# A 416-byte pad at the start of SBUF's left side in a one-core transformer layer

## Chip, core and metric

The kernel runs on one core of one Trainium2 chip. The metric is the device time of one execution in microseconds (us); a smaller number is better. The core's engines are TensorE (PE; its weight loads are shown apart as PEld), VectorE (DVE), ScalarE (ACT), GpSimd (POOL) and SyncE (SP, which issues most of the DMAs). SBUF, the on-chip memory, is addressed here by bytes within a partition; a tile takes the same bytes in all 128 partitions.

## The reference

One layer of a hybrid trunk, sequence 512, width 1024, all in float32:

```python
h = rms_norm(x, norm_mix)
proj = h @ w_in                       # 1024 x 8192: pool, lru, q, k, v, three gates
gates = sigmoid(g_logits + b_gate)
y_pool = pool_mixer(u_pool)           # causal means over 2/4/8/16, a map per group of 256
y_lru = rglru_mixer(u_lru)            # conv of width 4, two block-diagonal gates, a scan
y_sb = stick_breaking_attention(rms_norm(q), rms_norm(k), v)   # 8 heads of 128
merged = gates[0]*(y_pool @ w_branch[0]) + gates[1]*(y_lru @ w_branch[1]) \
       + gates[2]*(y_sb @ w_branch[2])
x = x + merged @ w_out
h2 = rms_norm(x, norm_ffn)
x = x + (silu(h2 @ w_ffn_gate) * (h2 @ w_ffn_up)) @ w_ffn_down   # d_ff 2816
```

## The kernel before

**Precision.** Every large product is done in split float32: each operand is the sum of a high part (rounded to the format float32r) and a low part (the rest), and TensorE does three matmuls, high by high, high by low and low by high, that add up in PSUM. A weight tile is loaded (`raw`, `qw` or `w`), ACT writes its high part (`whi` or `wh`, lines 92 and 1109), DVE subtracts and writes the low part (`wlo` or `wl`, lines 93 and 1110). The helper `mm3` (lines 215 to 218) issues the three matmuls; in the products of q, k, v line 654 does it, in the feed-forward part line 1119.

**A matmul's operands.** The first operand of `nc.tensor.matmul(ps, stationary, moving)` is loaded into the array beforehand; the second streams through it, 512 or 256 columns. In the profile an instruction reads `out<-moving,stationary`.

**Stages.** (1) Gates of branch 0 from the unnormalised input `hu`. (2) The normalised input is written as `HH` (high) and `HL` (low); gates of branch 1 and the lru projection, `HH`/`HL` moving. (3) q, k and v by a seven-product scheme (Strassen's kind), in which blocks of `HH`/`HL` (for three of the seven products) or of sums of them (`hT1` to `hT4`, for the other four) are stationary and the weights move; gates of branch 2 between. (4) The pool projection, with `HH`/`HL` moving, and the branch projections (`ps_br`), between which the attention of the eight heads is done in small tasks. (5) The last branch and the output projection (`ps_out`), whose moving operands are `mth` and `mtl`. (6) The feed-forward part: two chunks directly (`ps_fg`, `ps_fu`), seven more by seven 256-wide products each (`ps_y`, `ps_x`), then the down projection, partly direct (`ps_d`), partly by seven products (`ps_dy`, `ps_dx`).

**What sets the order.** The program is written out in order and each engine works its own queue. `weights()` makes the split weights ready three chunks ahead of their use; a list of small tasks (`bg`, `abg`) is worked off one or two at a time between half chunks. Semaphores keep data and buffers safe. No order depends on an address.

**Where buffers lie.** Tile pools are stacked. From the low end ("left") come the constants `cst`, then `mp`, `wp`, and above these `ap0` in stages 1 to 3, `sp` and `ap1` in stages 4 and 5, `gp` in stage 6. From the high end ("right") come `hp`, which holds `HH` and `HL`, and after it, in the same place, `cor`, which holds `mth` and `mtl` and later the raw weight tiles `w` and the normalised blocks `hn` of the feed-forward part. The places in the code, by line:

```python
# L67 to L72
    cst = ctx.enter_context(tc.tile_pool(name="cst", bufs=1))
    mp = ctx.enter_context(tc.tile_pool(name="mp", bufs=4))
    wp = ctx.enter_context(tc.tile_pool(name="wp", bufs=3))
    ...
    hp = hstack.enter_context(tc.tile_pool(name="hp", bufs=1, side="right"))
# L215 - L218
    def mm3(ps, lh, ll, rh, rl, start, stop, skip=False):
        nc.tensor.matmul(ps, lh, rh, start=start, stop=False, skip_group_check=skip)
        nc.tensor.matmul(ps, lh, rl, start=False, stop=False, skip_group_check=skip)
        nc.tensor.matmul(ps, ll, rh, start=False, stop=stop, skip_group_check=skip)
# L942
    cor = ctx.enter_context(tc.tile_pool(name="cor", bufs=8, side="right"))
```

The tiles of `mp`, `wp`, `ap0`, `sp`, `ap1`, `gp`, `hp` and `cor` are multiples of 512 bytes long, so all buffers of one side begin at the same residue modulo 512; in the built program this is 64 on the left and 480 on the right. The small tiles of `cst` (identity, ones, mask, scale columns) have residues of their own.

Of the kernel before, what the change touches and what calls it, by code (L numbers as in the profile page):

```python
# [8 lines left out]
F32 = mybir.dt.float32  # L9
# [7 lines left out]
P = 128  # L17
# [13 lines left out]
KD = 4  # L31
H = S // 2
AHEAD = 200
NAW, NAT, NAB = 8, 8, 13
NSP = 44
NLD = 12
# [24 lines left out]
def layer_kernel(ctx: ExitStack, tc: tile.TileContext, x, xt, vecs, w_in, w_pool, w_rg, w_ig,  # L61
# [5 lines left out]
    cst = ctx.enter_context(tc.tile_pool(name="cst", bufs=1))  # L67
# [131 lines left out]
    def emit_next():  # L199
# [4 lines left out]
        key, make = specs[i]  # L204
        with tc.high_priority(AHEAD if i > 3 else 0):
            ready[key] = make(str(i))
# [16 lines left out]
    def vcol(name, i=0):  # L223
        o = VOFF[name] + i
        return vt[:, o:o + 1]

    warm = cst.tile([P, S], BF16, tag="warm", name="warm")
    dve.memset(warm, 1.0)
    idn = cst.tile([P, P], F32, tag="idn", name="idn")
# [1077 lines left out]
```

## Time and profile before

| | us |
|---|---|
| median of 3 runs (lowest, highest) | 957.63 (956.97, 958.15) |
| the profiled execution's time | 956.69 |
| its span, first to last instruction | 954.9 |
| PE busy | 941.5 (99%) |
| PEld busy | 802.7 (84%) |
| DVE busy | 703.5 (74%) |
| ACT busy | 493.7 (52%) |
| POOL busy | 43.1 (5%) |

Busy times are shares of the span. PE's busy time is a union of modelled durations: a matmul is shown from its start to the end of its drain, and the next one starts before that, so the spacing of starts says more than the duration. In a row of instructions stand line, engine, operation, `out<-in`, shape and count, then the sum of busy time and the mean of one in ns, then idle time of the engine before them and what ended it. In a row of the timeline stand the start in us from the span's start, the duration in us, and the instruction. In the chain of work that ended last a piece has its start, its length, and the number of instructions merged in it. The granted TensorE clock was 0.999 of full speed over the span.

### The profile page before, as it was taken

How to read it: one execution, taken by the hardware profiler on the slowest of the kernel's cores; microseconds unless marked ns; L12 is line 12 of the kernel's file. 1: busy time of each engine (PE TensorE's matmuls, PEld its weight loads, DVE VectorE, ACT ScalarE, POOL GpSimd, SP SyncE). 2: the span in 40 equal slices, each digit the busy share in tenths (PEclk: the TensorE clock that was granted, in tenths of full speed). 3: DMA queues.
4: the chain of work that ended last, by engine and by line, in shares of the span. 5: the costliest groups of instructions: out<-in, count | busy, mean ns of one | idle time of the engine just before them, and what ended most of it. 6: DMA issues, size and time to landing. Idle time of an engine off the chain costs nothing.

```text
span 954.9 us, 13025 instructions
## 1 busy us (share of the span) xinstructions
PE 941.5 (99%) x5090; PEld 802.7 (84%) x5090; DVE 703.5 (74%) x876; ACT 493.7 (52%) x664; POOL 43.1 (5%) x71
## 2 busy tenths in 40 slices
PE   8899999999999999999999999999999999999998
PEld 5787778788888888788788878889999999988898
DVE  6597677978696599865865554699888887787464
ACT  5567779445755466654543223555555555652232
POOL 1100000131121000000000000000000000000000
PEclk9999999999999999999999999999999999999999
DMA  8474343661713933165432234345533334523001
GB/s 269 138 260 130 111 136 129 199 204 58 224 65 138 297 117 121 63 178 165 146 101 88 89 114 153 108 122 145 150 93 89 111 95 129 166 98 111 1 27 63
DMA packets 127790, 124.12 MB, mean 130 GB/s; under 512 B 7280, under 2 KB 107632, under 8 KB 127728
## 3 DMA queue, kind: packets, MB, share of 16 engines
q1 hardware_dynamic: 123840, 109.13, 36.9%
q0 software_dynamic: 3888, 14.16, 4.4%
q8 instruction: 40, 0.66, 0.3%
q14 instruction: 22, 0.18, 0.1%
HBM read 107.01 MB, written 16.25 MB: 129 GB/s over the span
## 4 chain that ended last, share of the span: by engine, by line
PE 91%; DVE 5%; ACT 2%; DMA 1%; issue 1%; SPq 0%; POOL 0%; DVEq 0%; ACTq 0%; POOLq 0%
PE ps_y L1119 11%; PE ps_q L654 9%; PE ps_x L1119 8%; PE ps_br L216 4%; PE ps_br L218 4%; PE ps_br L217 4%; PE ps_gate L217 4%; PE ps_gate L218 4%; PE ps_gate L216 4%; PE ps_d L216 3%; PE ps_d L218 3%; PE ps_d L217 3%; PE ps_dy L1119 2%; PE ps_dx L1119 2%; PE ps_out L216 2%; PE ps_lru L217 2%
## 5 line engine op out<-in xcount | busy, mean ns | idle before, releaser
L92 ACT ACTIVATE whi<-raw 128x1024 fp32r<-128x1024 f32 x93 | 98.3, 1058 | 159.0 <-PE ps_br L217 44.8
L93 DVE TENSOR_TENSOR wlo<-raw,whi 128x1024 fp32r<-128x1024 f32 x93 | 113.6, 1221 | 78.7 <-ACT whi L92 74.2
L1109 ACT ACTIVATE wh_S<-w_S 128x1024 fp32r<-128x1024 f32 x44 | 46.6, 1061 | 58.7 <-PE ps_y L1119 27.2
L1110 DVE TENSOR_TENSOR wl_S<-w_S,wh_S 128x1024 fp32r<-128x1024 f32 x44 | 53.6, 1221 | 13.7 <-ACT wh_S L1109 13.6
L1109 ACT ACTIVATE wh<-w 128x1024 fp32r<-128x1024 f32 x33 | 35.0, 1060 | 50.8 <-issue 13.4
L93 DVE TENSOR_TENSOR wlo<-qw,whi 128x1024 fp32r<-128x1024 f32 x36 | 43.9, 1221 | 20.5 <-ACT whi L92 20.2
L1110 DVE TENSOR_TENSOR wl<-w,wh 128x1024 fp32r<-128x1024 f32 x33 | 40.3, 1222 | 18.9 <-ACT wh L1109 18.9
L92 ACT ACTIVATE whi<-qw 128x1024 fp32r<-128x1024 f32 x36 | 38.0, 1056 | 30.4 <-PE ps_q L654 17.1
L216 PE MATMUL ps_gate<-HH,whi 128*128 128x512 f32 x128 | 50.9, 397 | 0.0
L218 PE MATMUL ps_gate<-HH,wlo 128*128 128x512 f32 x128 | 50.8, 397 | 0.0
L217 PE MATMUL ps_gate<-HL,whi 128*128 128x512 f32 x128 | 50.7, 396 | 0.0
L216 PE MATMUL ps_d<-ah,whi 128*128 128x512 f32 x112 | 43.6, 391 | 0.0
L217 PE MATMUL ps_d<-al,whi 128*128 128x512 f32 x112 | 43.6, 389 | 0.0
L218 PE MATMUL ps_d<-ah,wlo 128*128 128x512 f32 x112 | 43.6, 389 | 0.0
L1097 DVE TENSOR_TENSOR w_S<-w,w 128x1024 f32<-128x1024 f32 x22 | 26.9, 1222 | 3.4 <-PE ps_d L217 2.9
L218 PEld LDWEIGHTS ps_gate<-HH,wlo 128*128 128x128 f32 x128 | 24.1, 188 | 5.8
L217 PEld LDWEIGHTS ps_gate<-HL,whi 128*128 128x128 f32 x128 | 24.1, 188 | 5.7
L216 PEld LDWEIGHTS ps_gate<-HH,whi 128*128 128x128 f32 x128 | 24.1, 188 | 5.6
L1097 DVE TENSOR_TENSOR w_S<-w,w_S 128x1024 f32<-128x1024 f32 x22 | 26.9, 1223 | 0.6
L872 DVE TENSOR_TENSOR_SCAN E<-K,zero 128x511 f32<-128x511 f32 (+3 forms) x32 | 25.5, 813 | 1.5 <-ACT K L867 1.3
L216 PE MATMUL ps_out<-mth,whi 128*128 128x512 f32 x64 | 25.4, 398 | 0.9 <-DVE g L299 0.9
L216 PE MATMUL ps_gate<-hu,whi 128*128 128x512 f32 x64 | 25.2, 394 | 1.0 <-ACT whi L366 0.7
(638 smaller groups left out, 3047.8 us busy)
## 6 DMA issues: line engine op xcount, KB each, us to landing
raw<-in_w_in_dram SPq DMA_DIRECT2D x39, 512.0 KB, 4.1
qw<-in_w_in_dram SPq DMA_DIRECT2D x24, 512.0 KB, 4.6
raw<-in_w_branch_dram SPq DMA_DIRECT2D x24, 512.0 KB, 3.4
w<-in_w_ffn_gate_dram SPq DMA_DIRECT2D x36, 256.0 KB, 3.5
w<-in_w_ffn_up_dram SPq DMA_DIRECT2D x36, 256.0 KB, 4.2
raw<-in_w_ffn_down_dram SPq DMA_DIRECT2D x14, 512.0 KB, 3.5
qd<-r POOLq DMA_DIRECT2D x12, 512.0 KB, 3.4
at<-qd SPq DMA_DIRECT2D x24, 256.0 KB, 5.2
```

The costliest lines, as they stand in the source:

```text
L92: act(hi, raw, AF.Copy)
L93: dve.tensor_tensor(lo, raw, hi.bitcast(F32), ALU.subtract)
L216: nc.tensor.matmul(ps, lh, rh, start=start, stop=False, skip_group_check=skip)
L217: nc.tensor.matmul(ps, lh, rl, start=False, stop=False, skip_group_check=skip)
L218: nc.tensor.matmul(ps, ll, rh, start=False, stop=stop, skip_group_check=skip)
L654: nc.tensor.matmul(ps[:, a, :], b_[:, k, ts_], a_[:, kk, :], start=first and n == k == 0, stop=n == 2 and k == 3, skip_group_check=True)
L872: dve.tensor_tensor_scan(E[:, f - 1:c0 + n - 1][:, ::-1], K[:, f:c0 + n][:, ::-1], zero[:, 0:1].to_broadcast([P, c0 + n - f]), 1.0, ALU.mu ...
L1097: dve.tensor_tensor(t, raw[c, x], raw[c, y], op)
L1109: act(h, raw[c, nm], AF.Copy)
L1110: dve.tensor_tensor(l, raw[c, nm], h.bitcast(F32), ALU.subtract)
L1119: nc.tensor.matmul(o, a[:, w, k, :], b[:, k, :], start=first and n == k == 0, stop=n == 2 and k == 3, skip_group_check=True)
```

## The change

A tile of 104 float32 is taken from `cst` between the vector of parameters `vt` and the other constants. Nothing writes or reads it. All other constants and all left pools then lie 416 bytes higher; the right pools stay where they are. No instruction is added, removed or moved.

```diff
@@ constants at the top
 H = S // 2
 AHEAD = 200
+PAD = 104
 NAW, NAT, NAB = 8, 8, 13
@@ layer_kernel, after vt and vcol
         return vt[:, o:o + 1]
 
+
+    cst.tile([P, PAD], F32, tag="pad", name="pad")
     warm = cst.tile([P, S], BF16, tag="warm", name="warm")
     dve.memset(warm, 1.0)
     idn = cst.tile([P, P], F32, tag="idn", name="idn")
```

## The prediction

> **What bounds the kernel now.** I read the chain of waits first, then the chain in order of time, the groups of TensorE instructions with shapes kept apart, and the timeline of single matmuls. The first says who sets the end:
>
> ```profile
> PE 91%; DVE 5%; ACT 2%; DMA 1%; issue 1%; SPq 0%; POOL 0%; DVEq 0%; ACTq 0%; POOLq 0%
> ```
>
> TensorE (PE) carries 91% of the chain, and it hardly ever waits. Its longest waits, from the view of waits for PE:
>
> ```profile
> PE rbps L407 <- DVE dg L406: 2.8, 1, 2.8
> PE warm_ps L336 <- DVE warm L228: 1.5, 1, 1.5
> PE ps_q L654 <- ACT r L666: 1.3, 1, 1.3
> ```
>
> So the time is, nearly, a number of matmuls times the spacing of their starts. That spacing is what the change can touch, because the change moves addresses and nothing else: in the built program all five engines have the same instructions in the same order with the same waits.
>
> **What addresses there are.** In the built program every buffer of the left pools mp, wp, ap0, sp, ap1 and gp starts at 64 modulo 512, and every buffer of the right pools hp and cor at 480. Tile rows and the slices taken for matmuls are multiples of 512 bytes, so each matmul reads two operands, the moving and the stationary one, with residues 64/64, 480/64 or 64/480. Pairs with one operand on the right are those with HH or HL (hp) and with mth or mtl (cor). The timeline of PE (start in us, duration, instruction), first a stretch whose moving operand is HH/HL, then one with mth/mtl, then one with both operands on the left:
>
> ```profile
> 63.72 0.40 PE L216 MATMUL ps_lru<-HH,whi 128*128 128x512 f32 x1
> ...
> 66.29 0.39 PE L218 MATMUL ps_lru<-HH,wlo 128*128 128x512 f32 x1
> ```
> ```profile
> 564.75 0.39 PE L216 MATMUL ps_out<-mth,whi 128*128 128x512 f32 x1
> ...
> 567.09 0.39 PE L217 MATMUL ps_out<-mtl,whi 128*128 128x512 f32 x1
> ```
> ```profile
> 619.80 0.39 PE L216 MATMUL ps_fu<-h2h,whi 128*128 128x512 f32 x1
> ...
> 622.30 0.39 PE L218 MATMUL ps_fu<-h2h,wlo 128*128 128x512 f32 x1
> ```
>
> There are 11, 10 and 11 matmuls from the first to the last row: 2.57/11 = 233.6 ns, 2.34/10 = 234.0 ns and 2.50/11 = 227.3 ns. Same shape, same granted clock (1.00 in all these stages), no wait. In the products of q, k and v the right operand is the stationary one; the chain in order of time has them as merged pieces, 48 or 24 matmuls each, the first with HH/HL, the second with the left tiles hT:
>
> ```profile
> 157.68 11.20 PE ps_q L654 x48
> 179.95 5.45 PE ps_q0S L654 x24
> 652.61 2.87 PE ps_y L1119 x24
> ```
>
> 11.20/48 = 233.3 ns against 5.45/24 = 227.1 ns. The third piece is the 256-wide product, both operands on the left: 119.6 ns. So a pair with unequal residues costs about 6.5 ns more, whichever of the two operands is the one on the right. The groups show the same step in the mean duration, and give the counts:
>
> ```profile
> L216 PE MATMUL ps_gate<-HH,whi 128*128 128x512 f32 x128 | 50.9, 397 | 0.0
> L218 PE MATMUL ps_pool<-HH,wlo 128*128 128x512 f32 x64 | 25.4, 397 | 0.0
> L218 PE MATMUL ps_out<-mth,wlo 128*128 128x512 f32 x64 | 25.4, 396 | 0.0
> L218 PE MATMUL ps_lru<-HH,wlo 128*128 128x512 f32 x64 | 25.4, 396 | 0.0
> L218 PE MATMUL ps_d<-ah,wlo 128*128 128x512 f32 x112 | 43.6, 389 | 0.0
> L218 PE MATMUL ps_fg<-h2h,wlo 128*128 128x512 f32 x32 | 12.5, 389 | 0.0
> ```
>
> Is it the position on the right, or the relation of the two addresses? One more look at the timeline, where both operands are on the left and PE has just restarted after a stall:
>
> ```profile
> 14.37 0.40 PE L218 MATMUL ps_gate<-hu,wlo 128*128 128x512 f32 x1
> ...
> 16.69 0.39 PE L216 MATMUL ps_gate<-hu,whi 128*128 128x512 f32 x1
> ...
> 19.18 0.39 PE L218 MATMUL ps_gate<-hu,wlo 128*128 128x512 f32 x1
> ```
>
> The first ten intervals take 2.32 us, 232 ns each; the next eleven take 2.49 us, 226.4 ns each. With the same operands the stream runs slowly at first and then falls into a faster rhythm. This is what two streams do that hinder each other: the read of the moving operand and the load of the next weights, whose relative position in time settles at a place where they no longer collide. My reading is that the left pairs can settle because both streams start at the same residue, and that a right/left pair keeps a difference (96 or 416 bytes modulo 512) with which it can't.
>
> **The change, part by part.** The pad is 104 float32, 416 bytes a partition, never written or read. It stands in the pool that comes first on the left, so all left pools move from 64 to 480 modulo 512, the right ones stay at 480, and all large pairs become 480/480. It fits exactly: the top of ap1 moves from 196160 to 196576, where hp begins.
>
> The gain, if 480/480 behaves as 64/64 does. Moving operand on the right: each group comes as three rows (high by high, low by high, high by low), so 3 x 128 (gates 1 and 2 with HH) + 3 x 64 (pool) + 3 x 64 (lru) + 3 x 64 (out) = 960 matmuls. Each saves 233.9 - 227.3 = 6.6 ns: 6.3 us. Stationary operand on the right: for each of q, k and v three of the seven products use a block of HH/HL, 24 matmuls in each, 3 x 3 x 24 = 216; each saves 233.3 - 227.1 = 6.2 ns: 1.3 us. Together 7.6 us.
>
> What of it reaches the end? In the stages of gates, lru, q/k/v and out PE has no idle beyond the waits above, and their chain is PE throughout, so there it counts whole, as long as weights keep coming. Here is the table of stages (length, then busy us of PE, PEld, DVE, ACT, POOL, clock, DMA share, GB/s):
>
> ```profile
> 56.00:157.50 101.50, 101.50 (x433) 80.86 (x432) 73.26 (x80) 76.01 (x91) 5.08 (x7) 1.00 0.51 165
> 157.50:299.00 141.50, 140.18 (x607) 113.74 (x606) 113.35 (x138) 83.76 (x109) 27.00 (x23) 1.00 0.42 138
> 299.00:505.00 206.00, 204.34 (x1023) 165.84 (x1023) 153.61 (x240) 107.60 (x185) 2.55 (x5) 1.00 0.49 148
> 562.00:608.50 46.50, 45.62 (x195) 36.45 (x194) 22.69 (x29) 16.11 (x22) 0.00 (x0) 1.00 0.41 136
> ```
>
> DVE is busy 72% and 80% of the first two, 49% of the last; a stage shorter by 2 to 3% leaves it below 83%. The weights are split three chunks ahead, and that cover hides DVE, ACT and the loads; without it one late split (a DVE piece of 1.2 us) would be paid. The 192 pool matmuls (1.3 us of the gain) run between the attention tasks of the third stage, where the chain hops over DVE; half of their gain may only lengthen a wait, so I take off 0.6 us. Net gain 7.0 us.
>
> The other engines. ACT, DVE and the DMAs also see the new addresses. Rows with a right-side tile, then rows with left tiles alone, of the same shape:
>
> ```profile
> L425 ACT ACTIVATE HH<-xt 128x1024 fp32r<-128x1024 f32 x4 | 4.2, 1052 | 0.8 <-DVE xt L421 0.8
> L92 ACT ACTIVATE whi<-raw 128x1024 fp32r<-128x1024 f32 x93 | 98.3, 1058 | 159.0 <-PE ps_br L217 44.8
> L426 DVE TENSOR_TENSOR HL<-xt,HH 128x1024 fp32r<-128x1024 f32 x4 | 4.9, 1214 | 0.0
> L93 DVE TENSOR_TENSOR wlo<-raw,whi 128x1024 fp32r<-128x1024 f32 x93 | 113.6, 1221 | 78.7 <-ACT whi L92 74.2
> w<-in_w_ffn_gate_dram SPq DMA_DIRECT2D x36, 256.0 KB, 3.5
> at<-qd SPq DMA_DIRECT2D x24, 256.0 KB, 5.2
> ```
>
> Within 1% for ACT and DVE, and the load into the right side (w) is not slower than one into the left (at), so I take nothing for them; 1 us more per load would still lie behind the chunks ahead. The 144 transposes (pw x80, pq x64) pair data with the identity in the constants, 64 with 96 now and 480 with 0 after: unequal both times, unknown; by the 6.6 ns above at most 1.0 us either way, taken as 0.
>
> The sum against the profiled execution: span 954.9 - 7.0 = 947.9, its time 956.69 - 7.0 = 949.7. The median of the runs, 957.63, is 0.9 above the profiled time; from it the forecast is **950.6 us**. The own range of this case goes from 949.0 (whole 7.6 and 1.0 from the transposes) to 954 (half the gain).
>
> [...]
>
> **Rivals.**
> 1. *The absolute start decides* (slower). 480 is 32 modulo 64 and 64 is 0 modulo 64: every slow pair has an operand that is off a 64-byte boundary, whichever role it has, and no fast pair does. Then the pad takes the left side off the boundary too: the fast pairs become slow and the slow ones stay. Price: 1730 left pairs 512 wide (gates 0: 192, branches 576, down 336, fg and fu 192, q/k/v 288, the rest in attention and the pool and lru maps) x 6.6 ns = 11.4 us. The 1944 matmuls 256 wide are bounded from both sides by 6.6 ns more, +12.8 us, and by short unsettled runs in attention, which are 3 ns shorter than the settled ones, -5.8 us:
>
> ```profile
> L1119 PE MATMUL ps_x<-B021h,wh 128*128 128x256 f32 x72 | 20.4, 283 | 0.0
> L218 PE MATMUL z<-qkh,qkl 128*128 128x256 f32 x16 | 4.5, 280 | 0.0
> ```
>
>    These rows are the nearest, so I take 0: 957.6 + 11.4 = 969.0, from 963 to 982. It decides from the point where the alignment of one operand alone is enough to spoil the rhythm. For it: residue and alignment can't be told apart in this trace. Against it: the slow start at 14.37 us, with no operand off a boundary, already has the spacing of the slow pairs, so the slow spacing is that of an unsettled pair, not an extra fetch. [...]
> [...]
>
> **How the numbers follow.** Equal residues settle: 0.63, 949 to 954. Absolute start: 0.27, 963 to 982. Nothing: 0.10, 957.6. A measurement of this kernel tells about 0.2%, 1.9 us, from no change; the first case lies wholly beyond it, so faster 0.63, same 0.10, slower 0.27. The range from 948.5 to 970 holds the first case, the case of no change and about half of the slower one, up to its likeliest value; some 0.15 stays out above.
>
> **What would show it.** Right: ps_gate<-HH, ps_lru, ps_pool, ps_out and ps_q<-whi,HH rows fall from 396-399 to 389-390, their starts from 234 to 227 ns; ps_d, ps_fg and the L1119 rows keep 389 and 283. The stage of lru and gates (384 of the 960) ends some 2.5 us earlier, the kernel 7. Wrong by the absolute start: ps_d, ps_fg and ps_br rise to 396 and the HH rows stay. Wrong by side: no row moves. If the HH rows fall and the time doesn't, a wait has taken the gain, to be looked for at the splits in q/k/v.

## The result, and the profile after

| | before | after |
|---|---|---|
| median of 6 runs each, side by side (us) | 957.89 | 952.97 |
| lowest to highest | 956.97 to 959.4 | 950.68 to 953.92 |
| ratio, 95% interval | | 0.9942 (0.993 to 0.9954) |
| profiled execution (us) | 956.69 | 953.92 |
| its span (us) | 954.9 | 952.1 |
| mean granted clock in it | 0.999 | 0.996 |

The changed kernel is faster by 4.9 us, by the interval 4.4 to 6.7; forecast were 7.0 us and a time of 950.6. That is half a per cent, but the ranges of the two sets of runs don't meet. In its listing the lines lie 1 to 3 lower: L217 to L219 are the three matmuls of `mm3`, L657 the product of q, k and v, L669 the copy `r` of q's result, L1122 the 256-wide products.

First the groups of TensorE instructions of the changed kernel (busy us, mean ns of one, idle before):

```profile
L217 PE MATMUL ps_gate<-HH,whi 128*128 128x512 f32 x128 | 50.0, 391 | 0.0
...
L219 PE MATMUL ps_lru<-HH,wlo 128*128 128x512 f32 x64 | 24.9, 389 | 0.0
L219 PE MATMUL ps_out<-mth,wlo 128*128 128x512 f32 x64 | 24.9, 389 | 0.0
L219 PE MATMUL ps_d<-ah,wlo 128*128 128x512 f32 x112 | 43.6, 389 | 0.0
L657 PE MATMUL ps_q<-whi,HH 128*128 128x512 f32 x48 | 18.7, 389 | 0.0
```

The rows shown with a right-side operand had 396 to 399 ns before and have 389 to 391 now; `ps_d`, with both operands on the left, kept 389. The mean of a row also holds the long durations right after a stop (`ps_pool<-HH,whi` went from 405 to 400), so the starts say it more clearly. From the timeline of PE, the lru stretch and the out stretch:

```profile
63.73 0.39 PE L219 MATMUL ps_lru<-HH,wlo 128*128 128x512 f32 x1
...
66.22 0.39 PE L218 MATMUL ps_lru<-HL,whi 128*128 128x512 f32 x1
...
564.71 0.39 PE L217 MATMUL ps_out<-mth,whi 128*128 128x512 f32 x1
...
567.21 0.39 PE L219 MATMUL ps_out<-mth,wlo 128*128 128x512 f32 x1
```

In each stretch there are 11 intervals: 2.49/11 = 226.4 ns and 2.50/11 = 227.3 ns, where before had 233.6 and 234.0. The chain in order of time (start, length, instructions merged) shows the product with `HH`/`HL` as stationary operand and the 256-wide product:

```profile
156.93 10.88 PE ps_q L657 x48
...
649.79 2.87 PE ps_y L1122 x24
```

10.88/48 = 226.7 ns instead of 233.3, and 119.6 ns as before. So the spacing did what was forecast. Where the time went is seen with stage marks, the times at which stages begin. A query by tile gives, for each group, its durations (lowest, median, highest) and the first and last start in us. Before:

```profile
L216 PE MATMUL ps_lru<-HH,whi x64: 392/397/400, 56.0 to 128.5; 128*128 128x512 f32 x64
L654 PE MATMUL ps_q<-whi,HH x48: 398/399/399, 157.5 to 280.6; 128*128 128x512 f32 x48
L216 PE MATMUL ps_pool<-HH,whi x64: 392/397/479, 308.7 to 368.0; 128*128 128x512 f32 x64
L216 PE MATMUL ps_out<-mth,whi x64: 392/397/472, 563.3 to 607.6; 128*128 128x512 f32 x64
L216 PE MATMUL ps_fg<-h2h,whi x32: 389/389/397, 608.3 to 640.9; 128*128 128x512 f32 x32
```

After:

```profile
L217 PE MATMUL ps_lru<-HH,whi x64: 388/389/389, 57.8 to 128.4; 128*128 128x512 f32 x64
L657 PE MATMUL ps_q<-whi,HH x48: 388/389/389, 156.8 to 280.3; 128*128 128x512 f32 x48
L217 PE MATMUL ps_pool<-HH,whi x64: 389/389/480, 308.4 to 366.8; 128*128 128x512 f32 x64
L217 PE MATMUL ps_out<-mth,whi x64: 389/389/468, 561.9 to 604.8; 128*128 128x512 f32 x64
L217 PE MATMUL ps_fg<-h2h,whi x32: 389/389/398, 605.5 to 638.1; 128*128 128x512 f32 x32
```

And the kernel both256 of the experiments below, which has equal residues too (256 on both sides) and whose one execution had a mean granted clock of 1.000:

```profile
L219 PE MATMUL ps_lru<-HH,whi x64: 388/389/395, 55.2 to 125.8; 128*128 128x512 f32 x64
L659 PE MATMUL ps_q<-whi,HH x48: 388/389/389, 154.1 to 276.0; 128*128 128x512 f32 x48
L219 PE MATMUL ps_pool<-HH,whi x64: 389/389/480, 304.2 to 362.6; 128*128 128x512 f32 x64
L219 PE MATMUL ps_out<-mth,whi x64: 389/389/472, 557.7 to 600.6; 128*128 128x512 f32 x64
L219 PE MATMUL ps_fg<-h2h,whi x32: 389/389/397, 601.3 to 633.9; 128*128 128x512 f32 x32
```

The differences of first starts, against the prediction's gain for the matmuls that lie in the stretch (of the 192 in gates 2, 144 lie between the blocks of q, k and v and 48 in the pool stage):

| stretch (us) | before | both256 | after | gain by count |
|---|---|---|---|---|
| start to first lru | 56.0 | 55.2 | 57.8 | 0 |
| lru to q (384 moving) | 101.5 | 98.9 | 99.0 | 2.5 |
| q to pool (144 moving, 216 stationary) | 151.2 | 150.1 | 151.6 | 2.3 |
| pool to out (240 moving) | 254.6 | 253.5 | 253.5 | 1.6 |
| out to feed-forward (192 moving) | 45.0 | 43.6 | 43.6 | 1.3 |
| from there to the end of the span | 346.6 | 346.6 | 346.6 | 0 |
| span | 954.9 | 947.9 | 952.1 | 7.7 (the forecast added it up as 7.6) |

Between the two executions at a mean clock of 0.999 and 1.000 the span drops by 7.0 us. The profile of after is 4.2 us longer than that of both256, nearly all of it in two places: 2.6 before the lru stage and 1.5 in q/k/v. Waits of PE, after:

```profile
PE ps_q L657 <- ACT r L669: 1.8, 1, 1.8
PE rbps L410 <- DVE dg L409: 1.6, 1, 1.6
PE ps_gate L217 <- ACT whi L369: 1.5, 1, 1.5
```

Three windows of after (length; busy us of PE, PEld, DVE, ACT, POOL; then the granted clock, DMA share, GB/s):

```profile
12.70:16.10 3.40, 3.40 (x10) 2.62 (x9) 3.20 (x10) 3.01 (x5) 0.00 (x0) 0.51 0.80 258
183.40:186.80 3.40, 1.57 (x8) 0.97 (x7) 3.12 (x4) 3.40 (x5) 0.77 (x2) 1.00 0.98 313
186.80:190.20 3.40, 3.40 (x10) 2.62 (x9) 1.76 (x6) 0.97 (x2) 1.47 (x1) 0.50 0.87 310
```

And the start of the last stretch as a timeline:

```profile
185.96 0.50 PE L657 MATMUL ps_q<-whi,hT3h 128*128 128x512 f32 x1 [1.83 <-ACT r L669]
...
187.13 0.63 PE L657 MATMUL ps_q<-wlo,hT3h 128*128 128x512 f32 x1
187.56 0.63 PE L657 MATMUL ps_q<-whi,hT3l 128*128 128x512 f32 x1
```

PE waits 1.83 us, restarts, and 0.9 us later its clock is at half for 3.4 us: seven matmuls come 427 ns apart instead of 227 and one 367, which is 7 x 0.2 + 0.1 = 1.5 us. At 12.7 us, after the wait of 1.5 us for `whi`, the clock falls for 3.4 us too. Both are falls of the clock, not costs of an address: both256, with a mean clock of 1.000, has a wait of 1.9 us at the same place:

```profile
PE rbps L412 <- DVE dg L411: 2.0, 1, 2.0
PE ps_q L659 <- ACT r L671: 1.9, 1, 1.9
...
PE ps_gate L219 <- ACT whi L371: 0.6, 2, 0.3
```

Where the two waits differ can be read from the traces. In after the recorded clock changes only on steps of 3.41 us: its two falls, at 12.74 and 186.82, lie 51 such steps apart. The whole 1.83 us of waiting lie in one step, 183.40 to 186.82. In both256 a step ends in the middle of the wait, and PE is idle for 1.65 of its 3.41 us:

```profile
179.74:183.15 3.41, 1.76 (x8) 1.13 (x6) 3.41 (x4) 2.76 (x3) 1.25 (x2) 1.00 0.93 342
```

In before the wait of 2.78 us for `dg` is divided too, 1.00 us in the step from 32.34 and 1.78 in the step from 35.76, and the clock stayed at 1.00. That idle time within one step decides is a reading of these three cases; no run tested it, and the other fall in after, at 12.74, came after 1.50 us.

### The profile page after: what moved, and what is told of

Read it like the earlier page. It is cut to its first block, busy times and chain, and to the rows that moved or that the text cites. A ratio compares the mean times of both kernels' runs of the same rounds, so it can differ in the third digit from the quotient of the medians.

```text
span 952.1 us, 13025 instructions
## 1 busy us (share of the span) xinstructions
PE 938.0 (99%) x5090; PEld 805.2 (85%) x5090; DVE 703.3 (74%) x876; ACT 493.0 (52%) x664; POOL 43.1 (5%) x71
## 4 chain that ended last, share of the span: by engine, by line
PE 89%; DVE 5%; ACT 2%; issue 1%; DMA 1%; POOL 1%; SPq 0%; DVEq 0%; POOLq 0%; ACTq 0%
PE ps_y L1122 11%; PE ps_x L1122 8%; PE ps_q L657 8%; PE ps_br L217 4%; PE ps_br L219 4%; PE ps_br L218 4%; PE ps_gate L218 4%; PE ps_gate L217 4%; PE ps_gate L219 4%; PE ps_d L217 3%; PE ps_d L218 3%; PE ps_d L219 3%; PE ps_dy L1122 2%; PE ps_dx L1122 2%; PE ps_out L217 2%; PE ps_lru L219 2%
## 5 line engine op out<-in xcount | busy, mean ns | idle before, releaser
L93 ACT ACTIVATE whi<-raw 128x1024 fp32r<-128x1024 f32 x93 | 98.4, 1058 | 153.9 <-PE ps_br L218 44.8
L94 DVE TENSOR_TENSOR wlo<-raw,whi 128x1024 fp32r<-128x1024 f32 x93 | 113.6, 1221 | 75.2 <-ACT whi L93 71.0
L1113 DVE TENSOR_TENSOR wl_S<-w_S,wh_S 128x1024 fp32r<-128x1024 f32 x44 | 53.6, 1221 | 13.7 <-ACT wh_S L1112 13.7
L217 PE MATMUL ps_gate<-HH,whi 128*128 128x512 f32 x128 | 50.0, 391 | 0.0
L219 PE MATMUL ps_gate<-HH,wlo 128*128 128x512 f32 x128 | 49.9, 390 | 0.0
L217 PE MATMUL ps_d<-ah,whi 128*128 128x512 f32 x112 | 43.7, 391 | 0.0
L218 PE MATMUL ps_d<-al,whi 128*128 128x512 f32 x112 | 43.6, 390 | 0.0
L219 PE MATMUL ps_d<-ah,wlo 128*128 128x512 f32 x112 | 43.6, 389 | 0.0
L217 PE MATMUL ps_gate<-hu,whi 128*128 128x512 f32 x64 | 26.5, 414 | 2.3 <-ACT whi L369 1.5
L219 PEld LDWEIGHTS ps_gate<-HH,wlo 128*128 128x128 f32 x128 | 24.0, 188 | 5.0
L217 PEld LDWEIGHTS ps_gate<-HH,whi 128*128 128x128 f32 x128 | 24.0, 188 | 4.9
L218 PE MATMUL ps_gate<-hu,whi 128*128 128x512 f32 x64 | 26.5, 414 | 0.0
```

What stands on the lines that cost most here:

```text
L93: act(hi, raw, AF.Copy)
L94: dve.tensor_tensor(lo, raw, hi.bitcast(F32), ALU.subtract)
L1113: dve.tensor_tensor(l, raw[c, nm], h.bitcast(F32), ALU.subtract)
```

## The experiments

Theory A: the relation of the two operands' starts decides (equal is fast). Rival B: the absolute start decides. Rival C: the right end of SBUF itself is slow. A second question followed: where do the missing microseconds go, into the wait for `r` in q or into the clock? Every edit is shown against the changed kernel, by its main lines.

**The relation set from the other side: right64.** No pad on the left; 416 bytes on the right, so both sides lie at 64.

```diff
+    rp = ctx.enter_context(tc.tile_pool(name="rp", bufs=1, side="right"))
+    rp.tile([P, 104], F32, tag="rpad", name="rpad")
     hp = hstack.enter_context(tc.tile_pool(name="hp", bufs=1, side="right"))
-    cst.tile([P, PAD], F32, tag="pad", name="pad")
```

> The left pad is gone; instead 416 bytes are taken at the top of the right side, so that hp and cor start at 64 modulo 512 like the left pools, which stay where they were before. Theory (the relation of the two residues decides): all pairs are 64/64, the HH, HL, mth and mtl matmuls are spaced 227 ns as with 480/480, ps_q with HH too, and the time falls as it did with the left pad, by 4 to 7 us against before. Rival (it was the start 480 of the left side, not the equality): the HH matmuls keep 234 ns and the time stays within 1 us of before.

Measured: median 952.0 us (951.27 to 953.15, 4 runs), ratio to before 0.9942 (0.9922 to 0.9963), the same as the change. The groups:

```profile
L219 PE MATMUL ps_gate<-HH,whi 128*128 128x512 f32 x128 | 50.0, 391 | 0.0
L221 PE MATMUL ps_out<-mth,wlo 128*128 128x512 f32 x64 | 24.9, 389 | 0.0
```

Moving the right side to the left's residue does what moving the left to the right's did. The start at 480 is not needed, and tiles at the right end are not slow in themselves. This speaks against B and C.

**A third common start: both256.** Left pad of 192 bytes, right pad of 224, so that both sides lie at 256.

```diff
-PAD = 104
+PAD = 48
+    rp = ctx.enter_context(tc.tile_pool(name="rp", bufs=1, side="right"))
+    rp.tile([P, 56], F32, tag="rpad", name="rpad")
```

> Left pad of 192 bytes and right pad of 224: both sides start at 256 modulo 512, a multiple of 256. Theory: as with 64/64 and 480/480, 227 ns everywhere. Rival (the absolute start has a part of its own, a common start on a larger boundary is better still): the settled spacing of 512-wide pairs falls below 226.7 ns, or that of 256-wide ones below 120 ns.

Measured: 949.68 us in one run; spacing 10.88/48 = 226.7 ns in q, as after. A common start on a 256-byte boundary is no faster than one at 480 or 64.

**How equal must they be: d256, d128, d64, d32.** The pad is changed alone, to leave a difference of 256, 128, 64 or 32 bytes between the sides.

```diff
-PAD = 104
+PAD = 40    # d256; 72 in d128, 88 in d64, 96 in d32
```

> Left pad of 160 bytes: left 224, right 480, a difference of 256 modulo 512. If the residues have to be equal modulo 512: HH, mth and HH-stationary matmuls stay near 234 ns and their mean durations at 396 or so. If equality modulo 256, 128 or 64 is enough: 227 ns and 389-390.

> Left pad of 288 bytes: left 352, right 480, a difference of 128 modulo 512. Equality modulo 64 or 128: 227 ns and 389-390. Equality modulo 256: 233-234 ns and 395-397.

> Left pad of 352 bytes: left 416, right 480, a difference of 64 modulo 512. If equality modulo 64 is what is needed, the HH, HL, mth and mtl matmuls fall to 227 ns and durations of 389-390, as with the differences 0 and 256; if it is modulo 128 or 256 they stay at 233-234 ns and 395-397.

> Left pad of 384 bytes: left 448, right 480, a difference of 32 modulo 512, hence also modulo 64, 128 and 256. Every form of the theory says slow, 231 to 235 ns; the rival that a pair is spoilt in proportion to its distance says nearly 227 ns, since 32 is the smallest step.

Measured, one run each: 953.85, 958.08, 956.62 and 957.68 us (before on the same chips: 957.73 with d256 and d32, 958.27 with the other two). The groups of d256:

```profile
L219 PE MATMUL ps_out<-mth,wlo 128*128 128x512 f32 x64 | 24.9, 389 | 0.0
L657 PE MATMUL ps_q<-whi,HH 128*128 128x512 f32 x48 | 18.7, 389 | 0.0
```

of d128:

```profile
L219 PE MATMUL ps_out<-mth,wlo 128*128 128x512 f32 x64 | 25.3, 395 | 0.0
L657 PE MATMUL ps_q<-whi,HH 128*128 128x512 f32 x48 | 19.0, 395 | 0.0
```

of d64:

```profile
L219 PE MATMUL ps_out<-mth,wlo 128*128 128x512 f32 x64 | 25.1, 392 | 0.0
L657 PE MATMUL ps_q<-whi,HH 128*128 128x512 f32 x48 | 18.9, 394 | 0.0
```

and of d32:

```profile
L219 PE MATMUL ps_out<-mth,wlo 128*128 128x512 f32 x64 | 25.3, 395 | 0.0
L657 PE MATMUL ps_q<-whi,HH 128*128 128x512 f32 x48 | 19.0, 396 | 0.0
```

A difference of 256 is as good as none. 32, 64, 128 and the 416 of before are slow. The mean spacing with `HH`, `HL`, `mth` or `mtl` moving, stops left out, is 234.1 ns in before, 233.3 with 32, 232.6 with 128, and 227.0 with 256 and with equal starts. 64 is a case between: 230.1 ns on the mean, with stretches of twelve matmuls at 229 and others at 233. In all of them `ps_d` keeps 389. Of the differences tried, those that are equal modulo 256 are fast and no others; equality modulo 512 is not needed, and equality modulo 128 is not enough.

**Can left pairs be made slow: gap416.** The pad is taken from its place and put between the pool `wp` and the pools above. Now `mp` and `wp`, with the split weights, lie at 64, and `ap0`, `sp`, `ap1`, `gp`, with the data, at 480, as do `hp` and `cor`: pairs of a weight and a data tile that were equal become unequal, on the left side alone.

```diff
     wp = ctx.enter_context(tc.tile_pool(name="wp", bufs=3))
+    gap = ctx.enter_context(tc.tile_pool(name="gap", bufs=1))
+    gap.tile([P, 104], F32, tag="gap", name="gap")
-    cst.tile([P, PAD], F32, tag="pad", name="pad")
```

> The 416 bytes lie between wp and the pools above it, not in the constants: mp and wp stay at 64, while ap0, sp, ap1 and gp move to 480, where hp and cor are. So the operands that shared a residue in the kernel before (weights in wp, activations in ap0, sp or gp) no longer do. Theory (relation): the 512-wide rows of ps_gate<-hu, ps_br, ps_d, ps_fg and ps_fu and those of q, k, v with hT rise from 389 to 396 and 227 to 234 ns; 1584 more matmuls at 6.6 ns are 10.5 us, so 968 if the 256-wide products pay nothing, 980 if each of their 1848 pays the same 6.6 ns. Rival (only an operand at the right end of SBUF is slow, equal residues cure just that): those rows stay at 389, the time near 957.8.

Measured: 963.2 us in one run (before in the same session: 958.58), span 961.4, 6.5 more than the profile of before. The groups:

```profile
L221 PE MATMUL ps_d<-ah,wlo 128*128 128x512 f32 x112 | 44.4, 396 | 0.0
L221 PE MATMUL ps_fg<-h2h,wlo 128*128 128x512 f32 x32 | 12.7, 396 | 0.0
```

and in the chain in order of time the 256-wide product that was 2.87 us before:

```profile
661.74 2.81 PE ps_y L1123 x24
```

`ps_d` and `ps_fg`, which no right-side tile touches, rise from 389 to 396. That ends rival C. The expected size (968, or 980) was missed: the 256-wide products do not stay as they are, they get *faster*, 2.81/24 = 117.1 ns instead of 119.6. Over all 1848 of the feed-forward part the mean is 117.3 instead of 120.0, 2.7 ns less.

For the sum one more row is needed: in this execution the clock fell at 38 us, and in the profile of before it didn't.

```profile
38.13:41.54 3.41, 3.10 (x11) 2.87 (x12) 1.73 (x6) 0.00 (x0) 0.00 (x0) 0.50 0.19 43
```

So compare from the first `ps_lru` on, behind the fall: from 58.9 to the end are 902.5 us, against 898.9 in before, 3.6 longer. By count, the 288 left pairs of q, k and v, 576 of the branches, 192 of `ps_fg` and `ps_fu` and 336 of `ps_d`, 1392 x 6.6 ns = 9.2 us, less 1848 x 2.7 ns = 5.0, make 4.2 us; what the other 0.6 is stays open. Of the 2.9 us ahead of lru, 192 gate pairs are 1.3; the rest fits the fall, half of 3.4 us.

**The wait in q: sqpool_after and sqpool_before.** PE waits for the copy `r` on ACT, and ACT comes from the square of the first q block. That one square goes to GpSimd, in the changed kernel and in the one before (where the pad is taken out as well).

```diff
+                if (t, i, j) == (0, 0, 0):
+                    nc.gpsimd.tensor_tensor(sq, r, r, ALU.mult)
+                else:
+                    act(sq, r, AF.Square)
-                act(sq, r, AF.Square)
```

> The changed kernel, and the square of the first finished block of q is done by GpSimd instead of ScalarE, so that the copy of ps_q that the third product S3 of q waits for is not queued behind it. Theory (part of the gain is taken back in q/k/v, where PE now waits longer for ACT, 1.8 us at that copy, and the clock falls to half for 3.4 us after it): the wait falls below 0.5 us, the granted clock stays 1.0 through the q products, and the time falls by 1 to 3 us below the changed kernel's 952 to 953, to some 950.5. Rival (the clock's fall there is chance and the wait is hidden by the next one): 952 to 953 as before; or DVE waits for the slower square and PE pays it at the next weights.

> The same move of one square to GpSimd, in the kernel before (no pad). There the wait was 1.3 us and the clock did not fall, so the theory expects less than in the changed kernel: 0.5 to 1.3 us below 957.8. If it gains as much here as there, the wait is no part of why the changed kernel gained less than 7 us.

Measured: sqpool_after 952.04 us (951.66 to 952.21, 5 runs), ratio 0.9929 (0.9916 to 0.9942); sqpool_before 958.15 (956.11 to 960.98, 12 runs), ratio 1.0 (0.9988 to 1.0013). Waits of PE in sqpool_after:

```profile
PE rbps L410 <- DVE dg L409: 2.8, 1, 2.8
...
PE ps_q L660 <- DVE wlo L94: 1.3, 2, 1.1
```

The wait for `r` (1.8) is gone, and behind it stands one for the low part of a weight (1.3, the longest 1.1): q is limited there by the splits, and removing one wait shows the next. Both expectations were missed. In the kernel before nothing is gained, where 0.5 to 1.3 us were expected. In the changed one some 950.5 were expected; the interval overlaps with that of the change (0.993 to 0.9954), so a gain is not shown.

**Keeping PE at work in the wait for `dg`: keepwarm_before, keepwarm_after, best.** Eight bf16 matmuls of the constant `warm` into the same PSUM tile were to fill the wait at 35 us; best has the moved square as well, and keepwarm_before has no pad.

```diff
             dg = b4([2, S], "dg")
+            for _ in range(8):
+                nc.tensor.matmul(ps, warm[:, 0:P], warm, start=True, stop=True)
```

> The kernel before, with eight bf16 matmuls of constants ahead of the broadcast of the row norms, where PE waits 2.8 us for DVE at 35 us; they fill that wait and their result is overwritten. Theory (the clock's fall to half for 3.4 or 6.8 us after that wait is a part of the spread, and differs from run to run): the granted clock no longer falls there, the time falls from 957.8 by 0.5 to 2 us on the median, and the spread of the runs narrows. Rival (the fall is not set off by that wait): same median and spread, or slower by up to 1.7 us, the time of the eight.

> The changed kernel with the same eight matmuls. If the clock is what made the change gain 4.9 us where 7.0 were forecast, the difference to the kernel before with the same eight is 6 to 7.5 us and the median 949.5 to 951. If the rest was lost to waits alone, the difference stays at 5 us.

> The changed kernel with both: the eight matmuls in the wait at 35 us, and the square of the first block of q on GpSimd, so that neither wait leaves PE idle for long. Theory: no fall of the clock in either place, 949 to 950.5 us, below the changed kernel by 2 to 3 us. Rival (the square only moves the wait to DVE's next weights): as the kernel with the eight alone.

Measured: keepwarm_before 960.48 us (958.84 to 962.15, 12 runs), ratio 1.0019 (1.0008 to 1.003); keepwarm_after 954.53 (952.92 to 955.75, 7 runs), 0.996 (0.9945 to 0.9976); best 953.61 (952.96 to 955.07, 6 runs), 0.9951 (0.9936 to 0.9965). The timeline of PE in keepwarm_before:

```profile
33.92 1.90 PE L407 MATMUL rbps<-warm 128*128 128x512 bf16 x8
...
38.65 1.15 PE L411 MATMUL rbps<-dg,ones 128*128 128x128 f32 x8 [2.83 <-DVE dg L410]
```

and its window right after that:

```profile
39.60:43.00 3.40, 3.40 (x10) 2.65 (x9) 3.13 (x5) 0.99 (x1) 0.00 (x0) 0.50 0.00 0
```

The eight took 1.90 us, but `dg` came at 38.65 instead of 37.54 in the profile of before, so PE still waited 2.83 us, and the clock fell to half all the same. Whether the filler delayed `dg` isn't shown. The theory that filler in this place keeps the clock up fell, and keepwarm_before is slower than before (1.0008 at least). keepwarm_after and keepwarm_before differ by 954.53 - 960.48 = -5.95 us, so the pad is worth about as much beside the filler. keepwarm_after (949.5 to 951 expected, if the clock was the reason) and best (949 to 950.5) missed their times; as the clock kept falling, they don't settle what it cost. No version beat the changed kernel beyond its interval (both256's 949.68 is below after's lowest, 950.68, but it is a single run at full clock).

## Why the prediction was right, and where its sizes were off

**The central step, equal starts settle.** Right, and shown from four sides: after (480/480), right64 (64/64), both256 (256/256) and d256 (224/480) have 227 ns; the differences of 32, 64, 128 and 416 have 230 to 234. The rows that were to fall did so, and those that were to stay stayed. That the two streams "hinder each other" and settle where they "no longer collide" was the author's reading of the step from 232 to 226.4 ns; no run shows it. The runs show that the relation of the two starts goes with 227 or with 230 to 234 ns, not by which mechanism.

**The gross gain, 7.6 us.** The stages of lru and gates 1 (2.6 measured in both256 for 2.5 by count) and of out (1.4 for 1.3), where all counted matmuls bear on the end, confirm it and come out slightly above. The saving of one matmul had been read from stretches of 10 and 11 intervals; over all intervals without a stop it is 234.1 - 227.0 = 7.1 ns for the moving pairs and 233.4 - 226.8 = 6.6 for the stationary, so the gross gain is 960 x 7.1 + 216 x 6.6 ns = 8.2 us.

**"There it counts whole" for q, k and v: the step that failed.** In both256 this stretch got only 1.1 us shorter of 2.3. By its starts the spacing alone gained 2.6, and 1.4 of it went into longer stops of PE, at four places. The first is the copy `r`: it begins on ACT 28.1 us after the first `ps_q` in before (185.65) and in both256 (182.30) alike, so what PE gains ahead of it turns into a longer wait, from 1.3 to 1.9 us (0.5 more). The other three are short stops in front of a matmul that reads a `wlo`, at 235.5, 271.4 and 277.1 us, together 0.9 us longer than the same intervals in before. Each of these matmuls starts when DVE has just written that `wlo`; here the second, from the timelines of DVE and PE of both256:

```profile
270.11 1.22 DVE L96 TENSOR_TENSOR wlo<-qw,whi 128x1024 fp32r<-128x1024 f32 x1
...
271.38 0.50 PE L659 MATMUL ps_q<-wlo,HH 128*128 128x512 f32 x1 [0.20 <-DVE wlo L96]
```

So both covers that the forecast had counted on fell short: the wait of 1.3 us on ACT already stood among the three longest, and three times the splits on DVE weren't ahead of PE, though DVE was busy only 80% of the stage. Here these waits on ACT and DVE took 1.4 of the 2.6 us that PE had gained ahead of them. sqpool_after shows the same limit: with the wait for `r` gone, PE waits 1.1 us for a `wlo`.

**The 0.6 us taken off in the pool stage.** Measured 1.6 - 1.1 = 0.5 in both256. The size was right; what took it stays open.

**What wasn't in the sum.** A gain of 0.8 us before the lru stage in both256 (the wait for `dg` was 2.0 us instead of 2.8), on which no counted matmul bears. In the kept profiles that wait goes from 1.6 to 4.1 us, so 0.8 is within what executions differ by. So the net forecast of 7.0 was met in that pair (0.8 + 2.6 + 1.1 + 1.1 + 1.4 = 7.0) partly by luck: the 1.2 that was lost in q/k/v is nearly made up by this 0.8 and by 0.1 each in the lru, pool and out stages. The waits were longer than forecast, and chance hid it.

**The clock.** The forecast took it as equal. In the profile of after one fall cost 1.5 us in q, where the profile of before had a clock of 1.00 through the whole stage, and the other about half of its 3.4 us, an estimated 1.7 of the 2.6 us ahead of lru. The rest isn't divided up: the wait for `whi` is 1.5 us there instead of 0.6, that for `dg` 1.6 instead of 2.0, and the first matmuls still come 427 ns apart up to 8.9 us. The clock varies from run to run in every kernel: the mean clock was 0.999 or more in 10 of 42 runs of the kernel before and in 2 of 11 of after, right64 and both256. Compared at like clock over these runs, the difference of the means is 956.9 - 950.2 = 6.7 us at 0.999 and above (10 and 2 runs), 958.6 - 952.5 = 6.1 at 0.998 (18 and 4), 959.02 - 953.06 = 5.96 at 0.996 (13 and 3). So the 4.9 us between the medians is partly the draw of the runs, but the interval (up to 6.7) leaves 7.0 out. Whether a shorter spacing makes falls likelier on the whole isn't settled: 2 in 11 and 10 in 42 can't be told apart. In q the traces suggest that it does: the wait for `r` is 1.0 to 1.3 us in the six traces with a slower spacing and that wait, and none fell there; it is 1.8 or 1.9 in the five with the fast spacing, and two of them (after and keepwarm_after, 1.8 each) fell.

**Costs taken as nothing.** The transposes `pw` and `pq` have 277 and 275 ns, 276 and 275 before; ACT's high part stays at 1058 ns, DVE's low part at 1221, the loads of `w` take 3.6 us (3.5), those of `at` 5.2 as before. All are confirmed at nearly nothing.

**Rival 1, the absolute start.** Its mark was `ps_d` at 396; it stayed at 389, and right64, both256 and d256 are fast at 64, 256, 224 and 480. The 256-wide rows that were to bound its cost had been read as a question of settling; gap416 shows that they follow the relation with the opposite sign (one run, one difference).

**No change, 957.6 (chance 0.10).** For this the right rows would have had to stay at 234 ns. They fell to 227 without any tile leaving the right end, and gap416 made slow pairs without it. The time fell to 952.97, and the pad had changed nothing but addresses.

## What to carry to other kernels

Where matmuls of one shape come at different spacings at the same granted clock and without waits, compare the SBUF starts of the moving and the stationary operand: for these 512-wide float32r products starts equal modulo 256 saved 6.6 to 7.1 ns each, 3%, at the price of an unused tile. Count such a gain whole only as far as the next wait on another engine, even a short one, since that wait can take back what was won ahead of it (1.4 us in q/k/v of both256); and compare executions of like clock before looking for a lost microsecond. In this kernel one arrangement is left untried: equal starts for the 512-wide pairs and unequal ones for the 256-wide feed-forward products, by gap416's rows an estimated 1848 x 2.7 ns = 5.0 us more.

## What was not expected of the hardware

- Of the differences tried only those that are 0 modulo 256 bytes were fast: with a difference of 256 the out rows have 389 ns, as with none, with 128 they have 395.
- The 256-wide products go the other way: on the mean 120.0 ns apart with equal starts, 117.3 with unequal ones (one run).
- After a PE wait of 1.8 us in q the clock was at half for 3.4 us (0.50 in the window), which cost 1.5 us; after one of 1.9 us at the same place in both256 it stayed at 1.00, and there 1.65 us of the wait lay in one step of 3.41 us. Eight filler matmuls of 1.90 us did not prevent a fall after the next 2.83 us of waiting.
- Why 256, and why the 256-wide products go the other way, stays open.
